# A hybrid HGRN2 and S5 block on one Trainium2 core: chunk scores in three products of 64 stationary columns, and the S5 output side ordered (step, channel)

## The chip, the cores and the metric

The kernel runs on one core of one Trainium2 chip. The metric is the device time of one execution in microseconds (us); the time before is the median of three executions. The matrix products run on TensorE (PE in the views, and PEld for its weight loads), elementwise work on VectorE (DVE), ScalarE (ACT) and GpSimd (POOL). SyncE (SP) issues nearly all transfers, in the order of its queue.

## The reference

The input is x, 2048 positions by 1024 channels in float32. One layer is computed:

```python
xn = rmsnorm(h, in_norm_g)
q, fz, v, gz, u = split(xn @ w_in)            # 4 x 512 for HGRN2, 512 for S5
# HGRN2, 4 heads of 128, chunks of 64 positions
b = cumsum(log f)                             # f from fz, k = 1 - f
q_dec, k_dec = q * exp(b), k * exp(-b)
att = where(lower triangle, einsum('ck,sk->cs', q_dec, k_dec), 0)
o = att @ v + q_dec @ s_start                 # s_start: state at the chunk's start
# S5: 32 groups of 16 channels, a diagonal complex state of 64 per group
x_t = abar * x_(t-1) + bbar @ u_t
y_t = Re(c @ x_t) + d * u_t
y = gelu(y); y = y * sigmoid(y @ w_glu + b_glu)
h = h + concat(o_hgrn, y_s5) @ w_out
h = h + conv_ffn(rmsnorm(h))                  # gated MLP, causal depthwise conv of width 3
out = rmsnorm(h)
```

All products are to float32 accuracy.

## The kernel before

**Stages.** The first stage, up to about 640 us, computes the input projection and, between its products, the HGRN2 and S5 mixers. It has 80 slots: two halves of 1024 positions, in each 20 blocks of 128 projection columns, for each two tiles of 512 positions (`tb`). The second stage, to about 900 us, has the S5 gate and the output projection; the rest is the MLP. The change touches the first stage alone.

**Projection.** A slot is one call of `project`: 24 products of 128 stationary columns by 512 moving ones (L220 to L222), because both operands are split into a high and a low part.

**Scores.** A `Unit` is one head for one tile of 512 positions, so there are 16. It holds four pairs of chunks (`i`). `kt` has three forms of the keys for a pair, 64 positions each: form 0 is the first chunk's keys, form 1 the same scaled for use by the second chunk's queries, form 2 the second chunk's own. `scores` (L633 to L647) makes for each pair the transposed scores: form 0 against the first chunk's queries into partitions 0 to 63, and forms 1 and 2 together, 128 stationary columns, against the second chunk's queries `qb[:, i, 2]` into all 128 partitions. VectorE then applies the mask to both parts (`attm`). The operands are plain float32, and one such product of the program appears as two records of TensorE in the trace.

**S5.** An `S5` object is one half of the positions for 64 channels (four groups in two pairs `j`): 8 for each half, 16 in all. Positions come in chunks of 8 steps (`TS`), and a tile has channel q (16) and step s (8) on its 128 partitions. `scan` (L481) runs the recurrence over chunks. `local_maps` makes `v`, the map from state to output, on VectorE; `kernel_rows` makes with it the 8-step impulse response by small products with 32 stationary columns (L551 to L554), writes it through DRAM (`m_d`) to get its shifted copies `mr`, and ScalarE reorders these into `mt` (L569). `output_map` forms the outputs from `mt` and `tv` (L576, L577), copies them to `ys`, and stores `ys` in `y_d` (L581). All this is made in the first half; in the second half `tv` and `mt` are read back from `tb_d`. `scan` has products of 64 stationary columns too (L489), which go in turn to partitions 0 to 63 and 64 to 127.

**Order.** A table of slots (`at`) says after which projection slot each step is recorded. A scheduling layer then sets the final order of each engine's instructions; each engine and SP's queue run theirs in that order.

Of the kernel before, what the change touches and what calls it, by code (L numbers as in the profile page):

```python
# [9 lines left out]
F32 = mybir.dt.float32  # L10
F32R = mybir.dt.float32r
I32 = mybir.dt.int32
AF = mybir.ActivationFunctionType
# [4 lines left out]
P = 128  # L18
# [23 lines left out]
def _bc(ap, dim, n):  # L42

    a = ap.unsqueeze(dim)
    shape = list(a.shape)
    shape[dim] = n
    return a.to_broadcast(shape)


def _body(ctx, tc, A, out, dbg=None):  # L50
    nc = tc.nc
    VE, SC, GP, PE = nc.vector, nc.scalar, nc.gpsimd, nc.tensor
    dma = nc.sync.dma_start

    def tt(eng, o, a, b, op):
        eng.tensor_tensor(o, a, b, op=op)  # L56

    def mul(o, a, b, eng=VE):
        eng.tensor_tensor(o, a, b, op=ALU.mult)

    def add(o, a, b, eng=VE):
        eng.tensor_tensor(o, a, b, op=ALU.add)  # L62

    def sub(o, a, b, eng=VE):
        eng.tensor_tensor(o, a, b, op=ALU.subtract)  # L65
# [7 lines left out]
    def stt(o, a, s, b, op0, op1, eng=VE):  # L73
        eng.scalar_tensor_tensor(o, a, s, b, op0=op0, op1=op1)  # L74
# [4 lines left out]
    y_d = dp.tile([512, TS, 2 * NCH], F32, name="y_d")  # L79
# [57 lines left out]
    with ExitStack() as p1:  # L137
# [4 lines left out]
        sp = p1.enter_context(tc.tile_pool(name="sp", bufs=1, side="right"))  # L142
# [147 lines left out]
        def cmul(o_re, o_im, ar, ai, br, bi, tmp, eng=VE, neg_im=False):  # L290

            mul(o_re, ar, br, eng)
            mul(tmp, ai, bi, eng)
            sub(o_re, o_re, tmp, eng)
            mul(o_im, ar, bi, eng)
            mul(tmp, ai, br, eng)
            if neg_im:
                stt(o_im, o_im, -1.0, tmp, ALU.mult, ALU.subtract, eng)
            else:
                add(o_im, o_im, tmp, eng)  # L300
# [21 lines left out]
        pw = [cs.tile([P, PAIRS, 9], F32, name=f"pw{i}") for i in range(2)]  # L322
# [12 lines left out]
        cre, cim = sbc[:, 0], sbc[:, 1]  # L335
# [104 lines left out]
        class S5:  # L440
# [79 lines left out]
            def local_maps(self):  # L520
                pq, bt, p0 = self.pq, self.bt, self.p0
                self.tv = sp.tile([P, 2, 2, P], F32, tag="tv", name="tv", bufs=2)
                if self.hf:
                    dma(self.tv.rearrange("p g j c -> p g (j c)"), tb_d[bt, 1].rearrange("p (g x) -> p g x", g=2))
                    return
                self.v = v = sp.tile([P, 2, 2, 16, 8], F32, tag="zi", name="v")
                tmp = sp.tile([P, 2, 16, 8], F32, tag="z2", name="ttmp2")
                cmul(v[:, 0], v[:, 1], _bc(pw[0][:, pq, 1:9], 2, 16), _bc(pw[1][:, pq, 1:9], 2, 16),
                     _bc(cre[:, pq], 3, 8), _bc(cim[:, pq], 3, 8), tmp, VE, neg_im=True)

                for g2 in range(2):
                    dma(tb_d[bt, 1].rearrange("(r n) (g x) -> g n r x", r=2, g=2)[g2],
                        v[g2 * 64 : (g2 + 1) * 64].rearrange("p r j q s -> p r (j q s)"))
                dma(self.tv.rearrange("p g j c -> p g (j c)"), tb_d[bt, 1].rearrange("p (g x) -> p g x", g=2))
                for i in range(2):
                    GP.tensor_copy(bd[i][0:64, :, 0:16], bb[i][0:64, pq])
                    GP.tensor_copy(bd[i][64:128, :, 16:32], bb[i][64:128, pq])

            def kernel_rows(self):

                pq, bt, p0 = self.pq, self.bt, self.p0
                self.mt = sp.tile([P, 2, 2, P], F32, tag="mt", name="mt")
                if self.hf:
                    dma(self.mt.rearrange("p g j c -> p (g j c)"), tb_d[bt, 3])
                else:
                    kp = ps_s5.tile([32, 2, P], F32, tag="s5", name="ps_k")
                    for j in range(2):
                        b0, b1 = bd[0][:, j], bd[1][:, j]
                        vr, vi = (self.v[:, r, j, :, 0:7].rearrange("p q s -> p s q") for r in range(2))
                        ko = kp[:, j, 16:128].rearrange("p (s q) -> p s q", q=16)  # L550
                        PE.matmul(kp[:, j, 0:16], b0, cre[:, p0 + j], start=True, stop=False)  # L551
                        PE.matmul(kp[:, j, 0:16], b1, nci[:, p0 + j], start=False, stop=True)
                        PE.matmul(ko, b0, vr, start=True, stop=False)
                        PE.matmul(ko, b1, vi, start=False, stop=True)  # L554
                    kr = sp.tile([32, 2, 256], F32, tag="kr", name="kr")
                    GP.memset(kr[:, :, 0:128], 0.0)
                    SC.activation(kr[:, :, 128:256], kp, AF.Copy)
                    dg = sp.tile([32, 2, 16], F32, tag="dg", name="dg")
                    mul(dg, _bc(dsk[:, pq], 2, 16), _bc(eye, 1, 2))
                    add(kr[:, :, 128:144], kr[:, :, 128:144], dg)  # L560

                    m = m_d[bt]
                    dma(bass.AP(m.tensor, m.offset, [[8 * (MS - 16), 32], [MS, 8], [1, 512]]),
                        _bc(kr.rearrange("p j x -> p (j x)"), 1, 8))
                    mr = sp.tile([P, 2, 2, 8, 16], F32, tag="kr", name="mr")
                    for g2 in range(2):
                        dma(mr[:, g2].rearrange("p j s q -> p j (s q)"),
                            bass.AP(m.tensor, m.offset + 128 + g2 * 128 * (MS - 16), [[MS - 16, P], [256, 2], [1, P]]))
                        SC.activation(self.mt[:, g2].rearrange("p j (q s) -> p j s q", q=16), mr[:, g2], AF.Copy)  # L569
                    dma(tb_d[bt, 3], self.mt.rearrange("p g j c -> p (g j c)"))  # L570

            def output_map(self):
                y = ps_s5.tile([P, 2, 2, NCH], F32, tag="s5", name="ps_y")
                for j in range(2):
                    for g2 in range(2):
                        PE.matmul(y[:, j, g2], self.mt[:, g2, j], self.ug[:, 2 * j + g2], start=True, stop=False)  # L576
                        PE.matmul(y[:, j, g2], self.tv[:, g2, j], self.x[:, g2, j], start=False, stop=True)  # L577
                ys = sp.tile([P, 2, 2, NCH], F32, tag="ys", name="ys")
                SC.activation(ys, y, AF.Copy)
                c0 = 64 * self.bt  # L580
                dma(y_d[c0 : c0 + 64, :, self.cq].rearrange("(g p) s c -> (p s) g c", g=4),  # L581
                    ys.rearrange("p j g c -> p (j g) c"))


        inj = hp.tile([P, 8, 64], F32, name="inj")
# [3 lines left out]
        class Unit:  # L589
# [43 lines left out]
            def scores(self):  # L633
                pa = ps_od.tile([P, 4, P], F32, tag="od", name="ps_att")
                kt, qb = self.kt, self.qb
                for i in range(4):
                    PE.matmul(pa[0:64, i, 0:64], kt[:, i, 0], qb[:, i, 0], start=True, stop=True)
                    PE.matmul(pa[:, i, 64:128], kt[:, i, 1:3].rearrange("p b t -> p (b t)"), qb[:, i, 2],  # L638
                              start=True, stop=True)
                am = attms[self.tb]  # L640
                tt(VE, am[0:64, :, 0:64].bitcast(I32), pa[0:64, :, 0:64].bitcast(I32),
                   _bc(mask[0:64, 0:64], 1, 4), ALU.bitwise_and)
                tt(VE, am[:, :, 64:128].bitcast(I32), pa[:, :, 64:128].bitcast(I32),
                   _bc(mask[:, 64:128], 1, 4), ALU.bitwise_and)
                self.ks = hp.tile([P, 4, P], F32, tag="ks", name="ks")
                for i in range(4):
                    SC.activation(self.ks[:, i], kt[:, i, 1:3].rearrange("p b t -> p (b t)"), AF.Copy, scale=self.e2[:, i])  # L647
# [100 lines left out]
        for hf in range(2):  # L748
# [12 lines left out]
            for bt in range(8):  # L761
                s0 = 40 * hf + 10 + (27 * bt + 6) // 8
                b = S5(hf, bt)
# [33 lines left out]
        for hf in range(2):  # L797
            for n in range(40):
# [31 lines left out]
                if cb < 4:  # L830
                    if cb % 2 == 0:
                        ut = sp.tile([P, 2, TS, 64], F32, tag="wt", name="ut", bufs=2)
                    t = ut[:, cb % 2]
                    pv = ps.rearrange("p (c s) -> p s c", s=TS)
                    mul(t, pv, rx[tb].rearrange("p (c s) -> p s c", s=TS))
                    c0 = hf * NCH + tb * 64
# [249 lines left out]
    for b in range(4):  # L1086
# [4 lines left out]
        else:  # L1091
# [6 lines left out]
            rows = [token_rows(0, q, ps_s5, "s5", hn) for q in range(4)]  # L1098
# [33 lines left out]
    with ExitStack() as p3:  # L1132
        pa = p3.enter_context(ExitStack())
# [101 lines left out]
        rows = [token_rows(1, q, ps_c, "x") for q in range(4)]  # L1235
# [309 lines left out]
        for n in range(NS):  # L1545
            c = n % 4
# [101 lines left out]
```

## Time and profile before

| | before |
|---|---|
| device time, median of 3 executions | 2277.9 us (2277.79 to 2279.31) |
| the profiled execution, its device time | 2280.0 us |
| its span, from the first to the last instruction | 2277.7 us |
| TensorE busy | 2194.5 us, 96% of the span |
| VectorE busy | 1700.9 us, 75% |
| ScalarE busy | 1006.0 us, 44% |
| chain that ended last: share of TensorE | 70% |
| mean granted TensorE clock | 0.985 of full speed |

A share of busy time is a mean over stages with different limits. Overlapping products count once in a busy time, and the ends of products are modelled, so the distance between two starts tells more than a duration does.

### The profile page before, as it was taken

What the parts mean: (1) busy time and instruction counts of PE and PEld (TensorE: products, weight loads), DVE (VectorE), ACT (ScalarE), POOL (GpSimd) and SP (SyncE); (2) the same over time, 40 slices, a digit from 0 to 9 for tenths busy, and PEclk for the clock granted to TensorE, in tenths of its full rate; (3) what the DMA queues carried; (4) which work ended last, traced back from release to release, by engine and by line L of the source; (5) the groups of instructions that cost most, each with busy time, mean ns of one, the idle gap of its engine ahead of it and who ended that gap; (6) DMA issues with size and microseconds to landing.
All of it is one profiled execution on the core that took longest, in us unless ns stands there. A gap on an engine that the chain in (4) does not pass through costs nothing.

```text
span 2277.7 us, 28419 instructions
## 1 busy us (share of the span) xinstructions
PE 2194.5 (96%) x10120; PEld 1764.9 (77%) x10120; DVE 1700.9 (75%) x2629; ACT 1006.0 (44%) x1834; POOL 730.3 (32%) x666
## 2 busy tenths in 40 slices
PE   8999999999989999899999999999999899999996
PEld 6678788888868886678788877888888677777775
DVE  9887787577655424877778798777777788788887
ACT  5343354232355335655555565555555423233343
POOL 1011100000000000554655556555554244444432
PEclk9899999999999999999999999999999999999998
DMA  6465555443424338434234234222221622222223
GB/s 226 139 222 171 178 178 155 143 144 121 153 74 139 114 117 261 137 124 134 83 125 153 84 131 147 76 82 84 83 84 65 231 84 93 66 92 75 75 83 120
DMA packets 169262, 287.33 MB, mean 126 GB/s; under 512 B 45857, under 2 KB 85665, under 8 KB 169121
## 3 DMA queue, kind: packets, MB, share of 16 engines
q1 hardware_dynamic: 164368, 268.23, 36.3%
q0 software_dynamic: 4752, 17.30, 2.0%
q8 instruction: 79, 1.29, 0.2%
q14 instruction: 63, 0.51, 0.1%
HBM read 191.11 MB, written 94.37 MB: 125 GB/s over the span
## 4 chain that ended last, share of the span: by engine, by line
PE 70%; DVE 17%; DMA 5%; issue 4%; ACT 3%; SPq 1%; POOL 1%; DVEq 0%; POOLq 0%; ACTq 0%
PE ps_u L1163 18%; PE ps_v L1163 9%; PE ps_out L964 7%; PE ps_pj L220 5%; PE ps_pj L222 5%; PE ps_du L1380 5%; PE ps_pj L221 5%; PE ps_w L1163 5%; PE ps_dv L1380 2%; DVE accp L62 2%; DMA graw<-gv_d 2%; PE ps_dn L1467 2%; DVE gvl L65 2%; PE ps_att L638 1%; DVE cv L74 1%
## 5 line engine op out<-in xcount | busy, mean ns | idle before, releaser
L220 PE MATMUL ps_pj<-xh,wh 128*128 128x512 f32 x640 | 262.1, 410 | 7.0 <-ACT xh L190 6.7
L221 PE MATMUL ps_pj<-xl,wh 128*128 128x512 f32 x640 | 256.6, 401 | 0.0
L222 PE MATMUL ps_pj<-xh,wl 128*128 128x512 f32 x640 | 256.2, 400 | 0.0
L74 DVE SCALAR_TENSOR_TENSOR cv<-cv,par 128x1024 f32<-128x1024 f32 x176 | 237.7, 1368 | 19.8 <-ACT cv L1175 17.9
L121 ACT ACTIVATE uh<-us 128x512 fp32r<-128x512 f32 x176 | 110.6, 630 | 182.7 <-PE ps_u L1163 89.1
L56 POOL TENSOR_TENSOR us<-uraw 128x512 f32<-128x512 f32 x86 | 122.0, 1419 | 185.5 <-DMA uraw<-in_wup_dram 172.5
L65 DVE TENSOR_TENSOR ul<-us,uh 128x512 fp32r<-128x512 f32 x133 | 151.9, 1142 | 3.1 <-ACT uh L121 2.9
L121 ACT ACTIVATE uh<-uraw 128x512 fp32r<-128x512 f32 x132 | 83.7, 634 | 159.5 <-PE ps_u L1163 83.9
L1380 PE MATMUL ps_du<-dh,gvh 128*128 128x512 f32 x320 | 131.5, 411 | 21.6 <-DVE accp L62 15.2
L220 PEld LDWEIGHTS ps_pj<-xh,wh 128*128 128x128 f32 x640 | 122.1, 191 | 37.6 <-ACT xh L190 6.7
L222 PEld LDWEIGHTS ps_pj<-xh,wl 128*128 128x128 f32 x640 | 121.8, 190 | 29.5 <-issue 1.1
L221 PEld LDWEIGHTS ps_pj<-xl,wh 128*128 128x128 f32 x640 | 121.9, 190 | 28.2 <-issue 1.5
L65 POOL TENSOR_TENSOR ul<-us,uh 128x512 fp32r<-128x512 f32 x43 | 72.0, 1674 | 177.0 <-ACT uh L121 172.6
L1380 PE MATMUL ps_du<-dh,gvl 128*128 128x512 f32 x320 | 128.7, 402 | 0.0
L1380 PE MATMUL ps_du<-dl,gvh 128*128 128x512 f32 x320 | 128.1, 400 | 0.0
L121 ACT ACTIVATE gvh<-gs 128x512 fp32r<-128x512 f32 x80 | 50.5, 632 | 158.0 <-POOL gs L56 77.4
L62 DVE TENSOR_TENSOR accp<-accp,ps_du 128x1024 f32<-128x1024 f32 (+1 forms) x84 | 97.7, 1164 | 28.7 <-PE ps_du L1380 28.6
L1175 ACT ACTIVATE cv<-cv,par 128x1024 f32<-128x1024 f32 x88 | 109.8, 1247 | 16.0 <-DVE cv L62 14.7
L56 POOL TENSOR_TENSOR gs<-graw 128x512 f32<-128x512 f32 x38 | 58.5, 1541 | 157.3 <-DMA graw<-gv_d 157.3
L964 PE MATMUL ps_out<-wo,ogp 128*128 128x512 f32 x384 | 100.1, 409 | 0.9 <-DVE og L74 0.9
L1380 PEld LDWEIGHTS ps_du<-dh,gvh 128*128 128x128 f32 x320 | 61.4, 192 | 45.2 <-issue 23.7
L964 PE MATMUL ps_out<-wo,zp 128*128 128x512 f32 x384 | 92.7, 397 | 0.0
(434 smaller groups left out, 6097.3 us busy)
## 6 DMA issues: line engine op xcount, KB each, us to landing
uraw<-in_wup_dram SPq DMA_DIRECT2D x86, 512.0 KB, 3.6
gv_d<-cv SPq DMA_DIRECT2D x43, 512.0 KB, 2.6
graw<-gv_d SPq DMA_DIRECT2D x84, 256.0 KB, 3.3
wraw<-in_win_dram SPq DMA_DIRECT2D x24, 512.0 KB, 4.7
xt<-in_wdown_dram SPq DMA_DIRECT2D x44, 256.0 KB, 2.9
ws_d<-wh POOLq DMA_DIRECT2D x16, 512.0 KB, 3.4
ws_d<-wl POOLq DMA_DIRECT2D x16, 512.0 KB, 6.1
wh<-ws_d SPq DMA_DIRECT2D x16, 512.0 KB, 4.0
```

Of the source, the lines that this page charges most:

```text
L56: eng.tensor_tensor(o, a, b, op=op)
L62: eng.tensor_tensor(o, a, b, op=ALU.add)
L65: eng.tensor_tensor(o, a, b, op=ALU.subtract)
L74: eng.scalar_tensor_tensor(o, a, s, b, op0=op0, op1=op1)
L121: SC.activation(h, raw, AF.Copy)
L220: PE.matmul(ps, a, xh, start=(kt == 0), stop=False)
L221: PE.matmul(ps, a, xl, start=False, stop=False)
L222: PE.matmul(ps, b, xh, start=False, stop=(kt == KT - 1))
L964: PE.matmul(pss[nh], parts[lp][kt][:, tq], wo[rp][kt][:, nh * BLK : (nh + 1) * BLK], start=first, stop=last)
L1163: PE.matmul(ps, l, r[kt], start=(fresh and first), stop=end, skip_group_check=not fresh)
L1175: SC.activation(c, cin[:, 2 : HALF + 2], AF.Identity, scale=tap[2], bias=par[:, C_CB + cb : C_CB + cb + 1])
L1380: PE.matmul(ps[:, i], l[:, j, i * P : (i + 1) * P], r, start=(fresh and n == 0), stop=(n == 5), skip_group_check=not fresh)
```

## The change

Three things change; the mathematics does not.

1. `scores` makes three products for a pair of chunks, each with 64 stationary columns: form 0 into partitions 0 to 63 (columns 0 to 63), form 2 into partitions 64 to 127 (columns 64 to 127), form 1 into partitions 0 to 63 (columns 64 to 127).
2. The S5 output side has step outside and channel inside. `v` is stored as (step, channel), so that the moving operand of L553 and L554 is read in one piece, where it was read with a step of 8 elements. The shifted copies are loaded straight into `mt`, and the two ScalarE copies for each of the 8 units are gone.
3. Since a tile's partitions are now (step, channel), the store of `ys` is written as four transfers of 64 KB where it was one of 256 KB.

```diff
-                self.v = v = sp.tile([P, 2, 2, 16, 8], F32, tag="zi", name="v")
+                self.v = v = sp.tile([P, 2, 2, 8, 16], F32, tag="zi", name="v")
...
-                cmul(v[:, 0], v[:, 1], _bc(pw[0][:, pq, 1:9], 2, 16), _bc(pw[1][:, pq, 1:9], 2, 16),
-                     _bc(cre[:, pq], 3, 8), _bc(cim[:, pq], 3, 8), tmp, VE, neg_im=True)
+                cmul(v[:, 0], v[:, 1], _bc(pw[0][:, pq, 1:9], 3, 16), _bc(pw[1][:, pq, 1:9], 3, 16),
+                     _bc(cre[:, pq], 2, 8), _bc(cim[:, pq], 2, 8), tmp, VE, neg_im=True)
...
-                        vr, vi = (self.v[:, r, j, :, 0:7].rearrange("p q s -> p s q") for r in range(2))
-                        ko = kp[:, j, 16:128].rearrange("p (s q) -> p s q", q=16)
+                        vr, vi = (self.v[:, r, j, 0:7].rearrange("p s q -> p (s q)") for r in range(2))
+                        ko = kp[:, j, 16:128]
...
-                    mr = sp.tile([P, 2, 2, 8, 16], F32, tag="kr", name="mr")
                     for g2 in range(2):
-                        dma(mr[:, g2].rearrange("p j s q -> p j (s q)"),
+                        dma(self.mt[:, g2],
                             bass.AP(m.tensor, m.offset + 128 + g2 * 128 * (MS - 16), [[MS - 16, P], [256, 2], [1, P]]))
-                        SC.activation(self.mt[:, g2].rearrange("p j (q s) -> p j s q", q=16), mr[:, g2], AF.Copy)
...
-                dma(y_d[c0 : c0 + 64, :, self.cq].rearrange("(g p) s c -> (p s) g c", g=4),
-                    ys.rearrange("p j g c -> p (j g) c"))
+                for g in range(4):
+                    dma(y_d[c0 + 16 * g : c0 + 16 * (g + 1), :, self.cq].rearrange("p s c -> s p c"),
+                        ys[:, g // 2, g % 2])
...
-                    PE.matmul(pa[0:64, i, 0:64], kt[:, i, 0], qb[:, i, 0], start=True, stop=True)
-                    PE.matmul(pa[:, i, 64:128], kt[:, i, 1:3].rearrange("p b t -> p (b t)"), qb[:, i, 2],
-                              start=True, stop=True)
+                    for rows, cols, k, q in ((0, 0, 0, 0), (64, 64, 2, 2), (0, 64, 1, 2)):
+                        PE.matmul(pa[rows : rows + 64, i, cols : cols + 64], kt[:, i, k], qb[:, i, q],
+                                  start=True, stop=True)
```

On TensorE the second unit's scores stand inside a projection slot. Before, its four pairs are eight products of alternating size (`ps_att` is the score tile, `ps_pj` a projection's):

```order
L637 MATMUL ps_att<-qb,kt 64x64
L638 MATMUL ps_att<-qb,kt 128x64
L637 MATMUL ps_att<-qb,kt 64x64
L638 MATMUL ps_att<-qb,kt 128x64
L637 MATMUL ps_att<-qb,kt 64x64
L638 MATMUL ps_att<-qb,kt 128x64
L637 MATMUL ps_att<-qb,kt 64x64
L638 MATMUL ps_att<-qb,kt 128x64
L221 MATMUL ps_pj<-xl_367,wh 128x512
```

In the changed kernel the same place has twelve products of one size:

```order
L222 MATMUL ps_pj<-xh_365,wl 128x512
L220 MATMUL ps_pj<-xh_365,wh 128x512
L637 MATMUL ps_att<-qb,kt 64x64 x12
L221 MATMUL ps_pj<-xl_367,wh 128x512
L222 MATMUL ps_pj<-xh_365,wl 128x512
```

The place among the projection's products is the same; of the 16 units none moves by more than one projection product.

On SP's queue, this is a piece around the third unit of S5 before (`y_d` is the outputs in DRAM, `wraw` a block of projection weights, `og_d` HGRN2's outputs):

```order
L469 DMA ug<-u_d 128x4x128
L720 DMA og_d<-og 128x512
L581 DMA y_d<-ys 128x4x128
L567 DMA mr<-m_d 128x2x128 x2
L204 DMA wraw<-in_win_dram 128x1024
L570 DMA tb_d<-mt 128x512
L480 DMA tb_d<-tw 128x512
```

And this is the same piece in the changed kernel (its lines are 1 or 2 lower from here on):

```order
L469 DMA ug<-u_d 128x4x128
L719 DMA og_d<-og 128x512
L566 DMA mt<-m_d 128x2x128 x2
L580 DMA y_d<-ys 8x16x128 x4
L568 DMA tb_d<-mt 128x512
L204 DMA wraw<-in_win_dram 128x1024
L480 DMA tb_d<-tw 128x512
```

The store of `ys` is four transfers, the load of `mt` stands ahead of it here, and the weight block stands behind both and behind the store of `mt`.

## Rows read from the trace of the kernel before

**Rows 1.** Windows: span, busy us (instructions) by engine, clock, DMA share, GB/s.

```profile
100.00:340.00 240.00, 238.09 (x1358) 190.27 (x1358) 191.75 (x494) 99.37 (x258) 24.60 (x71) 0.99 0.56 178
340.00:640.00 300.00, 299.28 (x1636) 246.44 (x1635) 194.28 (x445) 100.73 (x280) 2.18 (x15) 1.00 0.45 140
```

**Rows 2.** Waits of TensorE, 100 to 640 us: total us, times, longest.

```profile
PE ps_k L554 <- DVE v L74: 0.8, 1, 0.8
PE ps_att L637 <- DVE kt L59: 0.8, 1, 0.8
PE ps_att L637 <- ACT kt L622: 0.7, 1, 0.7
```

**Rows 3.** Timeline of TensorE, second unit's scores: start, us, what, records merged.

```profile
106.52 0.33 PE L637 MATMUL ps_att<-qb,kt 128*64 128x64 f32 x2
106.78 0.43 PE L638 MATMUL ps_att<-qb,kt 128*128 128x64 f32 x2
107.15 0.33 PE L637 MATMUL ps_att<-qb,kt 128*64 128x64 f32 x2
...
108.89 0.48 PE L221 MATMUL ps_pj<-xl,wh 128*128 128x512 f32 x1
```

**Rows 4.** Tile ps_att: weight loads, duration in ns min/median/max.

```profile
L637 PEld LDWEIGHTS ps_att<-qb,kt x128: 132/136/231, 93.1 to 628.6; 128*64 128x64 f32 x128
L638 PEld LDWEIGHTS ps_att<-qb,kt x128: 186/189/338, 93.5 to 628.9; 128*128 128x128 f32 x128
```

**Rows 5.** Timeline of TensorE, 124 to 127 us.

```profile
124.06 1.05 PE L682 MATMUL ps_ds<-vn,kst 128*128 128x128 f32 x8
124.95 0.60 PE L656 MATMUL ps_vn<-ident,vt 128*128 128x128 f32 x4
125.48 1.09 PE L489 MATMUL ps_b<-ug,tw 128*64 128x128 f32 x16
126.50 0.51 PE L220 MATMUL ps_pj<-xh,wh 128*128 128x512 f32 x1
```

**Rows 6.** Timeline of TensorE, 121 to 123 us: the impulse response.

```profile
121.74 0.23 PE L551 MATMUL ps_k<-sbc,bd 128*32 128x16 f32 x2
...
121.89 0.56 PE L553 MATMUL ps_k<-v,bd 128*32 128x112 f32 x2
122.27 0.59 PE L554 MATMUL ps_k<-v,bd 128*32 128x112 f32 x2
122.78 0.50 PE L221 MATMUL ps_pj<-xl,wh 128*128 128x512 f32 x1
```

**Rows 7.** Timeline of TensorE: the first unit's scores.

```profile
93.06 0.47 PE L637 MATMUL ps_att<-qb,kt 128*64 128x64 f32 x2
...
97.00 0.77 PE L222 MATMUL ps_pj<-xh,wl 128*128 128x512 f32 x1
```

**Rows 8.** Windows, as rows 1: three short stretches.

```profile
220.00:240.00 20.00, 19.24 (x99) 15.57 (x97) 19.88 (x49) 6.53 (x16) 1.79 (x5) 1.00 0.35 134
280.00:300.00 20.00, 19.97 (x123) 16.26 (x122) 19.69 (x65) 11.02 (x30) 2.33 (x6) 1.00 0.44 147
240.00:246.00 6.00, 6.00 (x29) 5.20 (x28) 6.00 (x12) 3.69 (x11) 0.53 (x1) 0.72 0.51 165
```

**Rows 9.** Timeline of TensorE: a unit's first product that waits.

```profile
238.45 0.33 PE L637 MATMUL ps_att<-qb,kt 128*64 128x64 f32 x2 [0.76 <-DVE kt L59]
```

**Rows 10.** Tiles mt, y_d, v and te: durations in ns min/median/max.

```profile
L569 ACT ACTIVATE mt<-mr x16: 655/730/797, 105.8 to 317.1; 128x256 f32<-128x256 f32 x16
L581 SPq DMA_DIRECT2D y_d<-ys x16: 370/371/1313, 119.3 to 639.2; - x16
L59 DVE TENSOR_TENSOR v<-pw,sbc x16: 408/419/426, 79.7 to 297.4; 128x256 f32<-128x256 f32 x16
L59 DVE TENSOR_TENSOR te<-f,e x16: 416/419/424, 80.4 to 293.7; 128x256 f32<-128x256 f32 x16
```

**Rows 11.** Waits of ScalarE, 100 to 640 us: total us, times, longest.

```profile
ACT wh L121 <- PE ps_pj L221: 54.7, 14, 7.3
```

More of the change, by code (lines that the diff above doesn't have):

```diff
@@ L525, in local_maps @@
                     return
-                self.v = v = sp.tile([P, 2, 2, 16, 8], F32, tag="zi", name="v")
-                tmp = sp.tile([P, 2, 16, 8], F32, tag="z2", name="ttmp2")
-                cmul(v[:, 0], v[:, 1], _bc(pw[0][:, pq, 1:9], 2, 16), _bc(pw[1][:, pq, 1:9], 2, 16),
-                     _bc(cre[:, pq], 3, 8), _bc(cim[:, pq], 3, 8), tmp, VE, neg_im=True)
+                self.v = v = sp.tile([P, 2, 2, 8, 16], F32, tag="zi", name="v")
+                tmp = sp.tile([P, 2, 8, 16], F32, tag="z2", name="ttmp2")
+                cmul(v[:, 0], v[:, 1], _bc(pw[0][:, pq, 1:9], 3, 16), _bc(pw[1][:, pq, 1:9], 3, 16),
+                     _bc(cre[:, pq], 2, 8), _bc(cim[:, pq], 2, 8), tmp, VE, neg_im=True)
                 for g2 in range(2):
                     dma(tb_d[bt, 1].rearrange("(r n) (g x) -> g n r x", r=2, g=2)[g2],
-                        v[g2 * 64 : (g2 + 1) * 64].rearrange("p r j q s -> p r (j q s)"))
+                        v[g2 * 64 : (g2 + 1) * 64].rearrange("p r j s q -> p r (j s q)"))
                 dma(self.tv.rearrange("p g j c -> p g (j c)"), tb_d[bt, 1].rearrange("p (g x) -> p g x", g=2))
```

## The prediction

> **What bounds the kernel now.** I first read the busy times by stretch, to see which engine the stage of the change belongs to. From 100 to 340 us TensorE is busy for 238.1 of 240 us, from 340 to 640 us for 299.3 of 300 [rows 1]. VectorE has 191.8 of 240 (80%) and 194.3 of 300 (65%), ScalarE 41% and 34%. Then I read the waits of TensorE in both stretches: three, 2.3 us in all [rows 2]. So TensorE sets the pace here, and each microsecond taken from its queue ends the stage earlier, as long as the other engines follow. [...] Since ends of products are modelled, I cost everything by distances between starts in the timeline.
>
> **Scores before.** One unit takes from 106.52 to 108.89, when the next projection product starts: 2.37 us [rows 3]. A pair of chunks takes 0.26 for the narrow product and 0.37 for the wide one, 0.63 us. All 15 units after 100 us lie in full-clock stretches like this one. The first lies in a stretch at half that clock, 93.06 to 97.00, 3.94 us [rows 7].
>
> **Scores after.** Twelve products, 24 records, all of 64 stationary by 64 moving columns. No row shows this shape in turns on the two halves of the output partitions, so I bound it by neighbours. L682, at full width, makes 8 records with 128 moving columns in 124.06 to 124.95, 0.111 us each; L489, with 64 stationary columns going to the halves in turn, makes 16 records of the same 128 moving columns in 1.02 us, changeover to the next work included [rows 5]. The halves thus run beside each other: each half has 8 records, at 0.109 us (the full-width distance, less a little) 0.87 us, which leaves 0.15 us for getting in and out. A load of 64 columns does not lengthen this: it is 53 ns shorter than one of 128 (136 against 189 ns) [rows 4], so 64 columns take some 53 ns, and L489 hides them under 0.109. With 64 moving columns a record takes half, 0.055 us, about one load. The change gives partitions 0 to 63 two products of three, 16 records: 16 x 0.055 + 0.15 = 1.03 us; the other half's 8 records lie beside them. Saved: 2.37 - 1.03 = 1.34 us a unit, 15 x 1.34 = **20.1 us**. The lower bound of the saving is L489's mean distance for all 24 records, 24 x 0.064 + 0.15 = 1.69 us, 0.68 saved a unit, 10.2 in all. I take the upper end, since L489's form is the change's own, with fewer moving columns.
>
> The first unit, at half clock, would take some 2.0 us and free 1.9. But projection products would then run in the freed time at half clock, where they take twice as long, so it is worth **1.0 us** (bounds 0 and 1.9).
>
> [...]
>
> **Impulse response.** L553 and L554 have 112 moving columns, read with a step of 8 elements. A pair of records takes 121.89 to 122.27, 0.19 us a record [rows 6], while 128 moving columns in one piece take 0.109 to 0.111 [rows 5]. In one piece 112 would take 112/128 of 0.109, 0.096 us: 0.095 saved. The 8 units of the first half have 8 such records each; the first unit waits for `v` anyway, so 56 records count: **5.3 us**. The bounds are 0, if not the step but the 32 stationary columns make them slow, and 5.3. I take 5.3, because L551, with the same 32 columns, stands at 0.037 and shows no floor. That row cannot rule out a lower rate per column. [...]
>
> **What costs nothing.** The 16 copies into `mt`, 0.73 us each [rows 10], leave ScalarE, which is 41% busy and which TensorE hardly waits for [rows 2]. The products for `v` on VectorE have the same 256 elements, and `te`, which has the new pattern of repeated operands, takes the same 419 ns [rows 10]. The store of `ys` issues 4 times, not once, at 0.37 us: 48 more issues, 17.8 us of SP's time, 1.1 us (up to 3.9 when an issue takes 1.31) in each of 16 places [rows 10]. Behind it in the queue stand weight blocks, `m_d` and `tv`. The cover is prefetch: ScalarE, which splits the weights, waits for TensorE to free the buffer (54.7 us, 14 times), and no wait of it for a weight block stands in these stretches [rows 11]. `mt` loses a copy of 1.5 us on its way, more than the delay. Without that cover the cost would be up to 17.8 us. The load of `mt` now itself waits until the unit before has been through L576; the copy that it replaces had that wait too.
>
> **What is lost again.** VectorE's work stays, while TensorE's saving in the first half is 7 x 1.34 + 5.3 = 14.7 us. On the mean VectorE goes from 80 to 85% there (192 of 225). Locally it is full: of the twelve 20 us stretches two have it above 98% [rows 8], two more above 90%. If what is saved inside full stretches goes into waits like the 0.76 us for `kt` [rows 9], two to four twelfths of 14.7 are lost, 2.4 to 4.9 us; I take **3.0**. In the second half, at 65%, nothing.
>
> **Sum.** 20.1 + 1.0 + 5.3 - 3.0 = 23.4 us. The profiled execution took 2280.0 us, a span of 2277.7 and 2.3 around it, so 2256.6 by its own measure. It stands 2.1 above the median of the runs, which gives 2254.5 there.
>
> **Rivals.** (All times on the median.)
>
> *Halves in turn.* If the halves do not run beside each other for products this short, 24 records take 24 x 0.055 + 0.15 = 1.47 us and save 0.90: 13.5 + 0.7 + 5.3 - 2.5 = 17.0, 2261. L489 speaks against it [rows 5].
>
> *The impulse response stays slow* (its bound of 0): 20.1 + 1.0 - 2.0 = 19.1, 2259.
>
> *VectorE takes over in the first half*, so that everything saved there turns into waits: 8 x 1.34 of the second half + 1.0 = 11.7, 2266. For it speak the full stretches [rows 8]; against it that VectorE is idle for 48 us of 240.
>
> *No gain from the scores.* If each change of half costs the drain that narrow to wide costs now (0.26 for a narrow product of two records, of which about 0.15 is the changeover), a pair takes 3 x 0.11 + 2 x 0.15 + 0.055 = 0.68 against 0.63, a loss of 3.5 us, with 5.3 - 1 gained: 2277. L489 changes halves seven times within 1.02 us and nearly excludes it.
>
> [...]
>
> **Chances.** The forecast 0.66, with its own range 2249 to 2260 (the first unit and the loss to VectorE at their bounds, a little in the record's distance); halves in turn 0.10; impulse response slow 0.08; VectorE 0.07; no gain from the scores 0.04; the clock 0.05. The range 2246 to 2266 takes in the first four, less some tails, and beyond the forecast's own low end the case that the fall of the clock at 241 us goes away (1.7 us). A change of 0.2%, 4.6 us, is about what a measurement of this kernel can tell: faster 0.91, same 0.04, slower 0.05.
>
> **What would show it.** In the trace after: a unit's scores from the first start to the next product near 1.03 us (1.47: halves in turn; 2.4 or more: drains); L553 to L554 0.19 us apart for a pair of records, where it was 0.38; the stage's end about 23 us earlier; waits of TensorE in 100 to 340 us of some 5 us, for `kt` and `v`; `ACT mt` gone; the granted clock as before. A wait for weights behind the four stores, or a lower clock around the scores, would make the prediction wrong.

## The result

The changed kernel takes 2250.6 us (median of 4 runs, 2248.4 to 2253.7) against 2277.85 for the kernel before (median of 4, 2272.6 to 2279.3): 27.3 us less, a ratio of 0.988 with a 95% interval of 0.986 to 0.989. Run again later beside other kernels it took 2254.2 us (6 runs) against 2279.0 (11 runs), 24.8 less, ratio 0.988 (0.986 to 0.990). The forecast was 23.4 less, 2254.5.

The windows of the changed kernel, over the two stretches that answer to [rows 1] and over the first microseconds of the mixers' stage (span, busy us by engine, clock, DMA share, GB/s):

```profile
100.00:320.00 220.00, 218.27 (x1402) 178.88 (x1401) 192.30 (x497) 90.08 (x242) 26.64 (x71) 1.00 0.62 196
320.00:610.00 290.00, 288.79 (x1696) 238.82 (x1696) 193.72 (x445) 100.21 (x279) 2.17 (x15) 1.00 0.47 144
87.00:101.00 14.00, 12.02 (x68) 9.10 (x69) 12.46 (x24) 6.28 (x19) 1.74 (x7) 0.76 0.50 128
```

TensorE is still busy for over 99% of both long stretches, which are taken 20 and 10 us shorter here. VectorE does the same work in less time: 87% in the first, where it had 80%. The third row matters below: the same 14 us of the kernel before have a clock of 0.52.

The waits of TensorE from 100 us to the stage's last projection product, near 621 us, the answer to [rows 2]:

```profile
PE ps_att L637 <- DVE kt L59: 0.7, 1, 0.7
PE ps_att L637 <- ACT kt L621: 0.7, 1, 0.7
PE ps_k L554 <- DVE v L74: 0.7, 2, 0.5
PE ps_pj L222 <- DMA wl<-ws_d: 0.5, 1, 0.5
PE ps_b L489 <- DMA ug<-u_d: 0.2, 1, 0.2
```

Together they are 2.8 us, 0.5 more than before. The last two, 0.7 us, are new in kind: waits for transfers. The waits for VectorE (for `kt` in L59 and for `v`) are 1.4 us, where they were 1.6.

The timeline of TensorE at the second unit's scores, then at the first unit's, then at the second unit's impulse response and at the stage's last projection product:

```profile
102.62 1.15 PE L637 MATMUL ps_att<-qb,kt 128*64 128x64 f32 x24
103.70 0.50 PE L221 MATMUL ps_pj<-xl,wh 128*128 128x512 f32 x1
...
93.83 1.21 PE L637 MATMUL ps_att<-qb,kt 128*64 128x64 f32 x24
94.97 0.50 PE L222 MATMUL ps_pj<-xh,wl 128*128 128x512 f32 x1
...
115.49 0.38 PE L554 MATMUL ps_k<-v,bd 128*32 128x112 f32 x2
115.71 0.21 PE L551 MATMUL ps_k<-sbc,bd 128*32 128x16 f32 x2
...
115.83 0.36 PE L553 MATMUL ps_k<-v,bd 128*32 128x112 f32 x2
116.03 0.35 PE L554 MATMUL ps_k<-v,bd 128*32 128x112 f32 x2
116.31 0.50 PE L220 MATMUL ps_pj<-xh,wh 128*128 128x512 f32 x1
...
620.55 0.40 PE L222 MATMUL ps_pj<-xh,wl 128*128 128x512 f32 x1
```

A unit's scores take 1.08 us where they took 2.37 [rows 3], the first unit's 1.14 where they took 3.94 [rows 7]. A pair of records of the impulse response takes 0.20 us where it took 0.38, and the last four of a unit, with the way out, 0.48 where they took 0.89 [rows 6]. The stage's last projection product starts at 620.55 us; before, it started at 650.15.

The stores of `ys`, the answer to the row of `y_d` in [rows 10] (ns min/median/max):

```profile
L580 SPq DMA_DIRECT2D y_d<-ys x64: 570/582/1246, 112.8 to 611.5; - x64
```

Each of the four is dearer to issue than the one was, 0.58 us against 0.37, so SP spends 37 us on them where it spent 6.

Since device times of one kernel differ by up to 12 us (2246.5 to 2258.4 in one set of six), the experiments are also compared by a stretch of the profile that holds the whole change and little else: from the start of the thirteenth projection slot, near 91 us, to the last projection product. I call it the mixer stretch. It is 559.6 us before and 529.2 after.

| kernel | device time, median | before beside it | ratio (95%) | mixer stretch |
|---|---|---|---|---|
| before | 2277.85 | | | 559.6, again 557.9 |
| changed | 2250.6 | 2277.85 | 0.988 (0.986 to 0.989) | 529.2, again 529.0 |
| scores alone | 2260.8 | 2278.8 | 0.992 (0.990 to 0.993) | 536.2 |
| S5 side alone | 2272.5 | 2278.8 | 0.997 (0.996 to 0.998) | 550.8 |
| narrow, then wide | 2263.8 | 2278.8 | 0.993 (0.992 to 0.994) | 541.0 |
| fourth product | 2249.8 | 2278.8 | 0.988 (0.986 to 0.990) | 529.3 |
| halves apart | 2253.8 | 2281.5 | 0.987 (0.985 to 0.990) | 533.2 |
| step of 2 | 2251.1, one run | 2281.5 | | 530.3 |
| step of 4 | 2251.1, one run | 2281.5 | | 534.3 |
| eight stores | 2254.9 | 2279.0 | 0.989 (0.988 to 0.991) | 530.1 |
| impulse response later | 2251.1 | 2279.0 | 0.988 (0.986 to 0.989) | 527.1 |

### The profile page after: what moved, and what is told of

It reads as the page before. It is cut to its first block, busy times and chain, and to the rows that moved or that the text cites. A ratio compares the mean times of both kernels' runs of the same rounds, so it can differ in the third digit from the quotient of the medians.

```text
span 2246.5 us, 28693 instructions
## 1 busy us (share of the span) xinstructions
PE 2163.2 (96%) x10248; PEld 1745.3 (78%) x10248; DVE 1700.3 (76%) x2629; ACT 994.9 (44%) x1818; POOL 732.3 (33%) x666
## 4 chain that ended last, share of the span: by engine, by line
PE 70%; DVE 17%; DMA 5%; issue 4%; ACT 3%; SPq 1%; POOL 1%; DVEq 0%; POOLq 0%; ACTq 0%
PE ps_u L1162 18%; PE ps_v L1162 9%; PE ps_out L963 7%; PE ps_du L1379 5%; PE ps_w L1162 5%; PE ps_pj L220 5%; PE ps_pj L222 5%; PE ps_pj L221 5%; PE ps_dv L1379 3%; DVE accp L62 2%; DVE gvl L65 2%; DMA graw<-gv_d 2%; DVE dl L65 1%; PE ps_dn L1466 1%; DVE cv L74 1%
```

## The experiments

**The parts alone.** The kernel before with the new scores only, and the changed kernel with the old scores:

```diff
-                    PE.matmul(pa[0:64, i, 0:64], kt[:, i, 0], qb[:, i, 0], start=True, stop=True)
-                    PE.matmul(pa[:, i, 64:128], kt[:, i, 1:3].rearrange("p b t -> p (b t)"), qb[:, i, 2],
-                              start=True, stop=True)
+                    for rows, cols, k, q in ((0, 0, 0, 0), (64, 64, 2, 2), (0, 64, 1, 2)):
+                        PE.matmul(pa[rows : rows + 64, i, cols : cols + 64], kt[:, i, k], qb[:, i, q],
+                                  start=True, stop=True)
```

Expected of the scores alone:

> The kernel before with the scores alone changed to three products of 64 stationary columns; the S5 output side stays (channel, step). Theory: the gain of the scores comes from two halves that run beside each other, 2.37 to 1.08 us a unit, 15 x 1.30 = 19.5 us, and 2 to 5 us more in the first unit and behind it, where the clock is at its lower level: 2253 to 2257 us. Impulse response still at 0.19 us a record. Rival (the S5 side carries more than its 5 to 6 us, through the shorter stretch at the lower clock or the freed ScalarE): 2260 us or more here, and the stretch at half clock after 87 us is still 13.7 us long.

Expected of the S5 side alone (the same edit, undone in the changed kernel):

> The changed kernel with the scores of before: only the S5 output side is in (step, channel) order. Theory: 56 records, each about 0.1 us shorter, 5 to 6 us: 2272 us, plus at most 3 if the stretch at half clock ends earlier; a unit's scores still 2.37 us, no wait of TensorE for SP's 48 more stores. Rival (the S5 side carries more): 2267 us or less. Rival (the stores cost something that the scores' gain hid): 2275 us or more.

Measured: the scores alone gain 18.0 us, a little less than expected and past the rival's limit of 2260 by less than the runs scatter; the rival's other sign, a stretch of 13.7 us at half clock, did not come (3.4 us, below). The mixer stretch gains 23.4. The S5 side alone gains 6.3 us (stretch 8.8), between the theory's 5 to 6 and its bonus for the clock. The sums, 24.3 and 32.2, come near the whole change's 24.8 to 27.3 and 30.4.

The sum of the stretches counts one gain twice, since each part alone brings the clock back earlier near 90 us (below). And the S5 side alone has two falls of the clock of its own, as its windows show (the clock is the number before the DMA share):

```profile
234.00:238.00 4.00, 4.00 (x18) 3.58 (x19) 4.00 (x9) 2.29 (x6) 0.53 (x1) 0.57 0.33 120
544.00:549.00 5.00, 5.00 (x32) 4.68 (x33) 4.89 (x8) 1.43 (x5) 0.00 (x0) 0.66 0.79 263
```

An estimate takes this out: half of the time at half clock (0.5 of full in the trace) is taken off each stretch (of 14.0 us before, 2.6 after, 1.0 with the scores alone, 9.2 with the S5 side alone); in the trace of the kernel before, projection products stand 0.43 us apart at half clock and 0.23 at full. The stretch then loses 16.9 us by the scores alone, 6.4 by the S5 side alone and 24.7 by both. So the scores carry about 70%, and neither part shows a cost that the other hides.

**Width changes or halves beside each other.** Two things set the new scores apart: all loads have one width, and two halves can run at once. In the kernel before, the narrow products were put first and the wide ones behind them:

```diff
                 for i in range(4):
                     PE.matmul(pa[0:64, i, 0:64], kt[:, i, 0], qb[:, i, 0], start=True, stop=True)
+                for i in range(4):
                     PE.matmul(pa[:, i, 64:128], kt[:, i, 1:3].rearrange("p b t -> p (b t)"), qb[:, i, 2],
                               start=True, stop=True)
```

> The kernel before with a unit's four narrow products first and then its four wide ones: the same eight products with one change of width where there were seven. Theory (width of the load and running beside each other count, changeovers only in part): narrow block 0.11 + 6 x 0.055 + 0.15 = 0.59 us, wide block 8 records at 0.11 and the way out, 1.07: 1.66 us a unit, 0.71 saved, 15 x 0.71 = 11 us: 2267 us. Rival (the changeovers are the whole gain of the three narrow products): about 1.1 us a unit, 20 us: 2257 us. Rival (changeovers cost nothing): 2.37 us a unit, 2278 us.

Its timeline at the second unit:

```profile
103.92 0.68 PE L637 MATMUL ps_att<-qb,kt 128*64 128x64 f32 x8
104.53 1.10 PE L639 MATMUL ps_att<-qb,kt 128*128 128x64 f32 x8
105.44 0.48 PE L221 MATMUL ps_pj<-xl,wh 128*128 128x512 f32 x1
```

The same eight products take 1.52 us, not 2.37: six changes of width fewer save 0.85, 0.14 us each. That is two thirds of what the three narrow products save (1.29), more than the 0.71 expected; the rest, 0.44 us, needs the narrow form. The starts of single records in the trace of the kernel before show the same price: after a change of width the first record comes 0.09 us and the second 0.05 us later than in a row of one width (narrow 0.151 and 0.107 apart in place of 0.058, wide 0.205 and 0.160 in place of 0.112). What TensorE does in such a change no run shows, so the drain that the forecast names is not shown either; measured is its price, 0.14 us, where the forecast had 0.15.

In the changed kernel a fourth product was then put into the quarter of the score tile that nothing reads (extra work, outputs unchanged):

```diff
-                    for rows, cols, k, q in ((0, 0, 0, 0), (64, 64, 2, 2), (0, 64, 1, 2)):
+                    for rows, cols, k, q in ((0, 0, 0, 0), (64, 64, 2, 2), (0, 64, 1, 2), (64, 0, 2, 0)):
```

> The changed kernel with a fourth product for each pair of chunks, into partitions 64 to 127, columns 0 to 63, which nothing reads: 16 records for each half instead of 16 and 8. Theory (halves beside each other, the longer half sets the time): a unit stays at 1.08 us and the time at that of the changed kernel, 2250 to 2252 us. Rival (halves take turns, or the issue of records is the limit): 8 records more at 0.04 to 0.055 us, 1.4 to 1.5 us a unit, 5 to 7 us more: 2256 to 2258 us.

```profile
103.45 1.15 PE L637 MATMUL ps_att<-qb,kt 128*64 128x64 f32 x32
104.53 0.50 PE L221 MATMUL ps_pj<-xl,wh 128*128 128x512 f32 x1
```

In this row of its timeline 32 records take the 1.08 us that 24 took. The halves do run beside each other, and the half with 16 records sets the time.

Last, the twelve products in another order, the eight for one half before the four for the other:

```diff
-                for i in range(4):
-                    for rows, cols, k, q in ((0, 0, 0, 0), (64, 64, 2, 2), (0, 64, 1, 2)):
+                for rows, cols, k, q in ((0, 0, 0, 0), (0, 64, 1, 2), (64, 64, 2, 2)):
+                    for i in range(4):
```

> The changed kernel with its twelve score products in another order: the eight for partitions 0 to 63 first, then the four for partitions 64 to 127. Theory (products start in the order of the queue, so the turns between the halves are needed): 16 + 8 records one behind the other, 24 x 0.055 + 0.15 = 1.47 us a unit in place of 1.08, 15 x 0.4 = 6 us: 2256 to 2257 us. Rival (each half has its own queue and its records pass those of the other): 1.08 us a unit, 2250 to 2252 us.

```profile
103.30 1.43 PE L637 MATMUL ps_att<-qb,kt 128*64 128x64 f32 x24
104.66 0.50 PE L221 MATMUL ps_pj<-xl,wh 128*128 128x512 f32 x1
```

1.36 us a unit, between the theory's 1.47 and the rival's 1.08: the turns are needed, but not for every record. In the trace the starts of single records make two rows, each with a step of 0.058 us once begun, and the row of the second half begins 0.17 us before that of the first ends. So, by these starts, three of its eight records ran beside the last three of the first half, ahead of their turn, and five came behind: 5 x 0.058 = 0.29, measured 0.28 us more. Over 15 units that is 4.2 us, and the mixer stretch is 4.0 longer (533.2 against 529.2). The device times alone would not show it.

**What slows the read.** Seven units' moving operand of the impulse response was copied by ScalarE into a tile where its elements stand 2 or 4 apart (for 4, two tiles with `t=4`):

```diff
+                if bt < 7:
+                    xt = x_tile()[:, 0:896].rearrange("p (r j x t) -> p r j x t", r=2, j=2, t=2)
+                    self.vs = [xt[:, 0], xt[:, 1]]
+                    for r in range(2):
+                        SC.activation(self.vs[r][:, :, :, 0], v[:, r, :, 0:7].rearrange("p j s q -> p j (s q)"), AF.Copy)
...
+                            vr, vi = (self.vs[r][:, j, :, 0] for r in range(2))
```

A pair of records takes 0.20 us with the operand in one piece, and took 0.38 with a step of 8. Expected for a pair with a step of 2:

> The changed kernel with the moving operand of L553 and L554 copied by ScalarE into a tile where it has a step of 2 elements (8 bytes), in seven of the eight units. [...] Rival (any step slows it): 0.38 us. The whole: within 3 us of the changed kernel, by the copy's delay before the product.

And with a step of 4:

> [...] Theory: a pair of records takes 0.38 us again, as with the step of 8 before, some 5 us more in all than with a step of 2. Rival (only a step beyond 16 bytes slows it, or it grows with the step): 0.20 us, or between.

The timeline at the second unit with a step of 2:

```profile
117.36 0.36 PE L561 MATMUL ps_k<-xt,bd 128*32 128x112 f32 x2
117.56 0.36 PE L562 MATMUL ps_k<-xt,bd 128*32 128x112 f32 x2
117.85 0.50 PE L222 MATMUL ps_pj<-xh,wl 128*128 128x512 f32 x1
```

And with a step of 4:

```profile
117.17 0.56 PE L560 MATMUL ps_k<-xt,bd 128*32 128x112 f32 x2
117.55 0.58 PE L561 MATMUL ps_k<-xt,bd 128*32 128x112 f32 x2
118.06 0.50 PE L222 MATMUL ps_pj<-xh,wl 128*128 128x512 f32 x1
```

A pair stands 0.20 us from the next with a step of 2, as in one piece, and 0.38 with a step of 4, as with the 8 of before. The mixer stretch differs by 4.0 us. The device times, one run each, are equal, so this rests on the rows and the stretch. It settles what [rows 6] left open: not the 32 stationary columns make these records slow, the read does. Why a step of 2 costs nothing and one of 4 does, no run shows.

**The clock near 90 us.** The kernel before was profiled again, unchanged:

> The kernel before once more, for its clock. In the profile of before the stretch at half clock after 87 us lasted 13.7 us, in five profiles of kernels with a part of the change 3.4 to 6.8. Theory (its length differs from execution to execution): 3.4 to 7 us here, and a device time of some 2274 to 2277 us. Rival (the wide scores and the slow impulse response keep the clock down): 10 us or more again.

The windows from 87 to 101 us, of the first and of the second profile of the kernel before:

```profile
87.00:101.00 14.00, 12.85 (x44) 9.26 (x45) 12.39 (x24) 5.72 (x18) 1.41 (x6) 0.52 0.43 114
```

```profile
87.00:101.00 14.00, 13.19 (x45) 9.55 (x46) 12.38 (x24) 5.68 (x18) 1.40 (x6) 0.51 0.45 121
```

The theory fell: the stretch at half clock was 13.7 us long again, while it is 3.4 with the scores alone and 6.8 in every other kernel here (row of the changed kernel above: 0.76). In all of them it begins near the end of a wait of TensorE of some 5 us for the first impulse response's operand (it begins at 87.5 us and the wait ends at 88.2 before; 87.2 and 89.0 in the changed kernel). So its length goes with the kernel: with either part changed, the clock is back 6.8 us earlier or more. That is 14 x (0.76 - 0.52) = 3.4 us of full speed. Which property of the work brings it back was not tried; neither narrower scores nor the faster read is needed, since the old products in another order (narrow, then wide) have 6.8 us too.

The fall at 241 us, 6 x 0.28 = 1.7 us of full speed [rows 8], is not in the second profile of the kernel before. But the three profiles with the old scores in the old order (the kernel before twice, the S5 side alone) have three such falls in the mixer stretch, at 241, 234 and 545 us, each at a unit's scores; the other ten have none. Whether the old scores bring them, or chance, is open.

**SP's queue.** Each store of 64 KB was cut in two:

```diff
                 for g in range(4):
-                    dma(y_d[c0 + 16 * g : c0 + 16 * (g + 1), :, self.cq].rearrange("p s c -> s p c"),
-                        ys[:, g // 2, g % 2])
+                    for s in range(2):
+                        dma(y_d[c0 + 16 * g : c0 + 16 * (g + 1), 4 * s : 4 * s + 4, self.cq].rearrange("p s c -> s p c"),
+                            ys[64 * s : 64 * s + 64, g // 2, g % 2])
```

> The changed kernel with eight stores of 32 KB for the outputs of a unit of S5 where it has four of 64 KB: 64 more issues on SP's queue. Theory (SP's time is covered by prefetch): 64 x 0.58 = 37 us more of SP's time, and the device time stays within 2 us of the changed kernel beside it. Rival (the queue is near its limit, as the one wait of 0.5 us for a weight block after the change suggests): 3 us or more, with waits of TensorE for weight blocks or for ug.

2254.9 us, beside 2254.2 for the changed kernel in the same set; the waits of TensorE from 100 us to the last projection product are 3.4 us in both, and the mixer stretch is 530.1 against 529.0. An issue of 32 KB took 0.50 us, so SP spent 27 us more, not 37. The cover holds.

**Impulse response later.** Since a change of width has a price, the impulse response of the first half was recorded one slot later, so that its products stand in fewer places:

```diff
-                at(s0 - 1, b.kernel_rows)
+                at(s0 - (hf == 1), b.kernel_rows)
```

> The changed kernel with the impulse response of a unit recorded one slot later in the first half, so that its products stand together: 9 places among the projection's products where there were 15 or so. Theory (each entry into narrow products and way out of them costs about 0.3 us, whatever lies between): 6 x 0.3 = 2 us less than the changed kernel beside it, and no wait for v (0.7 us). Rival (the later load of mt delays the output products): same or slower, with a wait of TensorE or SP for mt.

> The changed kernel itself once more, beside the two others. Theory: 0.988 of the kernel before; the stretch at half clock after 87 us 6.8 us long or less again; 27 us less than before, of which the profile gives 19.5 to the fifteen units of scores, 5.8 to the impulse response and 4 to 5 to the stretch at half clock. Rival (that stretch was short by chance): 13.7 us, and 3 us less gained.

The mixer stretch is 1.9 us shorter (527.1 against 529.0), near the 2 expected, though the products stand in 13 places where they stood in 17, and not in 9 for 15; TensorE no longer waits for `v` after 100 us, but 1.0 us for `vn`. The device time, 2251.1 against 2254.2 for the changed kernel beside it (ratios 0.988 each), cannot tell the two apart. The changed kernel's own second run repeats the first: stretch 529.0, half clock for 6.8 us.

## Why the prediction was right

**The scores.** Forecast 1.03 us a unit and 20.1 us in all; measured 1.08, so 15 x 1.29 = 19.4. The estimate of 0.055 us a record from L489 [rows 5] nearly holds: in the trace single records of one half start 0.058 us apart, and 16 x 0.058 + 0.15 = 1.08. One of the 15 units was not at full clock before, as the forecast had it: the fifth ran into the fall at 241 us. The reason was incomplete: two thirds of the saving come from changes of width, which the forecast named only in a rival (0.15 us of changeover) and did not use to explain the gain.

**The first unit.** Forecast 1.0 us (bounds 0 and 1.9); this term was mis-sized. I let the stretch at half clock stay as long as it was. It halved: in the profile the next slot starts 4.7 us earlier, counted from the beginning of the mixer stretch (8.83 us after it, where it was 13.55), 2.8 of it within the unit's scores and the rest in projection products at full clock, 0.23 us apart where they stood 0.43 apart at half clock (the forecast's factor of two was an estimate; this is 1.8). Among the chances the clock, at 0.05 and outside the range, stood for a loss only; it turned out a gain.

**The impulse response.** Forecast 5.3 us; the rows give 0.89 - 0.48 = 0.41 for four records with their way out, two such groups in each of 7 units: 5.7. That the step made them slow, and not the 32 columns, was the author's estimate from L551; the runs with steps of 2 and 4 showed it (0.20 and 0.38 us a pair). The 0.037 us of L551 is the mean of four records of the kernel before, its own and those of L552 behind them, between 121.74 and 121.89 us [rows 6]:

```profile
121.82 0.21 PE L552 MATMUL ps_k<-nci,bd 128*32 128x16 f32 x2
```

**Lost to VectorE.** Forecast 3.0 us; nothing was lost. TensorE's waits for VectorE are 1.4 us where they were 1.6 (1.8 in the second profile), and the 0.5 us by which all waits grew comes from the new waits for transfers. Why VectorE's full stretches cost nothing was not tried.

**At no cost.** The copies into `mt`, `v`'s products and the stores: none shows in the stretch. The price of an issue was too low (0.58, not 0.37), the cover was as said. One sign that the forecast named against itself came in small, a wait of 0.5 us for a block of weights (`wl`). But no store of `ys` stands in SP's queue in the 20 us before it, and the second profile of the changed kernel does not have it.

By rows the sum is 19.4 + 4.7 + 5.7 - 0.5 = 29.3 us, and the mixer stretch shows 28.8 to 30.7 (against either profile of before). Of that, 24.7 remain at full clock throughout (the estimate above); 4 to 6 us are the clock, which the forecast had only as a loss.

The device times show 24.8 to 27.3, with intervals that reach down to 23 and up to 31 us, so the two do not contradict each other. What scatters lies outside the stretch. Behind it the two profiles of the changed kernel, 0.2 us apart in the stretch, differ by 6.6 us; there half clock was granted for 50 and for 57 us, which explains at most 3.5 of them. Ahead of it the thirteenth slot starts at 90.2 and 90.5 us in the profiles of before and at 91.4 and 92.9 in those of the changed kernel. TensorE and SyncE run the same instructions in the same order up to there, and the kernel with the old products reordered, whose edit comes later, has 91.7; so this is not shown to come from the change, and its cause is open.

So the nearness of 2254.5 is in part luck: the first unit was sized too small by 3.7 us and the loss to VectorE too large by 2.5, both in the same direction, and the device times came out 2 to 5 us below the sum of the rows.

## What to carry to other kernels

Where small products with different stationary widths alternate, first count the changes of width: 0.14 us each here, more than a narrow product itself (two records, 0.12). Making all of one width, even with half as many instructions again, gained more than it cost (1.08 us a unit for 2.37), and products that go to the two halves of the output partitions should alternate in the queue to run at once (1.08 against 1.36 us; left apart, only three of eight records overlapped). The float32 moving operand of 112 columns was read as fast with a step of 2 elements as in one piece (0.20 us a pair of records); with a step of 4 or 8 the pair took 0.38. Other steps were not run.

## What the runs showed that was not expected

TensorE's clock after a wait of 5 us came back at 101 us in both profiles of the kernel before and at 92 to 96 in those of all other kernels; so what an edit saved there was worth more than its own length. And four transfers of 64 KB cost SP 0.58 us each to issue, and eight of 32 KB 0.50 each, where one of 256 KB, of as many rows in all, cost 0.37.
